# Narrow loads in four marked pieces and stores in halves, in a masked softmax that fills its DMA engines

## The chip, the cores and the metric

The kernel runs on one core of one Trainium2 chip. The metric is the device time of one execution in microseconds; lower is better. Each run has a state: slow, here, when it took over 1.5% longer than the fastest of its kernel, otherwise fast. A "ratio" is the mean time of one kernel's fast runs over the mean of the other's fast runs of the same rounds, so it is not quite the ratio of the medians quoted. The *span* of a profile is some 1.5 to 2.5 us shorter than the time measured for the same execution (154.3 against 155.95 us for the kernel before).

## The reference

```python
batch, heads, seq_q, seq_k = 16, 8, 256, 256       # x: float32; lengths: int, 128 to 255
for b in range(batch):
    length = lengths[b]
    masked = x[b, :, :, :length].copy()
    masked = masked - np.max(masked, axis=-1, keepdims=True)
    exp_masked = np.exp(masked)
    result[b, :, :, :length] = exp_masked / np.sum(exp_masked, axis=-1, keepdims=True)
# the rest of result is zero
```

A batch is 2048 rows of 256 floats: 2.10 MB in and 2.10 MB out. On chip it lies as 128 partitions of 16 rows. Only the first `length` columns of a row have to be read, but all 256 have to be written.

## The kernel before

Eight slots of 16 rows a partition hold the batches. Batches 0 to 3 are loaded whole by SyncE. Batches 4 to 15 are loaded by GpSimd, which reads the length, walks a tree of branches to the smallest width that covers it (160, 168, ... 240 or 256 columns), and issues one DMA of that width.

```python
slots = 8
ahead = 4
widths = list(range(160, 248, 8))
...
def parts(b):                       # how the store of batch b is cut
    if b == 0:
        cuts = [0, nt]              # nt = 16 rows a partition
    elif b < 8:
        cuts = [0, half, half + quarter, nt]
    elif b != batch - 3:
        cuts = [0, half, nt]
    else:
        cuts = [0, nt]
    return [slice(i, j) for i, j in zip(cuts, cuts[1:])]
...
for b in range(batch):              # SyncE: the stores
    s_b = s_st[b % 2]
    for s in parts(b):
        nc.sync.wait_ge(s_out, 2 * b + (s.stop - 1) // half + 1)    # divided
        if b >= 2 and s.start == 0:
            nc.sync.wait_ge(s_b, 64 * (b // 2 + 1))                 # store b-2 done
        nc.sync.dma_start(out=out_f[b, :, s, :], in_=xt[:, b % slots, s, :]
            ).then_inc(s_b, 16 * ((s.stop - s.start) // quarter))
...
with nc.Fori(0, (batch - ahead) // 2, 1, engines=[POOL]) as q:      # GpSimd: the loads
    for par in range(2):
        n = 2 * q + (ahead + par)
        v_len = length(POOL, word[0:1, bass.ds(2 * n, 1)])
        with nc.gpsimd.If(q >= 1):
            nc.gpsimd.wait_ge(s_sw[par], 16 * q)    # load n-2 has landed
            nc.gpsimd.wait_ge(s_st[par], 64 * q)    # store n-8 is done: the slot is free
        pick(v_len, bass.ds(n, 1), bass.ds(n % slots, 1), par, widths + [seq_k])
...
# VectorE: mask(b) waits for the load; ScalarE: exp with row sums, row by row;
# VectorE: divide(b, half) = reciprocal and multiply; a divided half may be stored
```

The softmax here doesn't subtract the row's maximum and nothing guards it: scores larger than these inputs give would overflow.

## Time and profile before

| | kernel before |
|---|---|
| time, median of 3 | 156.11 us (155.78 to 156.81) |
| span of the profiled execution | 154.3 us |
| DMA queues q0 (GpSimd's loads) and q1 (the rest), share of 16 engines' span | 32.2% and 66.0% |
| VectorE, ScalarE busy | 75%, 68% |
| VectorE's wait for loads | 14.0 us in all |
| last load landed (the last completion event of its semaphore) | 132.7 us |

The page's parts for this kernel are shown in the prediction. The list of waits of SyncE's queue, which issues the stores (who waits, on whom; us in total, times, longest):

```profile
SPq L119 <- DMA out_dram<-xt: 91.7, 14, 9.6
SPq L117 <- DVE xt L222: 14.9, 1, 14.9
SPq L120 <- DVE xt L222: 12.6, 9, 3.3
```

SyncE nearly always waits for an earlier store (91.7 us) and rarely for VectorE (12.6 us after the first batch). So there is a stock of finished batches that queue for the DMA engines. The end of the chain of waits (start in us, duration, what):

```profile
115.19 17.53 DMA xt<-in_x_dram
...
132.95 2.35 DVE xt L195
...
142.77 2.29 DVE xt L222
```

The last load, issued at 115.19 us, lands at 132.7; the mask and four multiplications follow, the last ending at 145.1 us. What lies between 145.1 and 154.3 is the rest of that stock being written. When the last load landed, 8.1 MB of the 33.6 MB of output was still to be stored (counted from the packet records).

### The profile page before, as it was taken

What the parts mean: (1) busy time and instruction counts of PE and PEld (TensorE: products, weight loads), DVE (VectorE), ACT (ScalarE), POOL (GpSimd) and SP (SyncE); (2) the same over time, 40 slices, a digit from 0 to 9 for tenths busy, and PEclk for the clock granted to TensorE, in tenths of its full rate; (3) what the DMA queues carried; (4) which work ended last, traced back from release to release, by engine and by line L of the source; (5) the groups of instructions that cost most, each with busy time, mean ns of one, the idle gap of its engine ahead of it and who ended that gap; (6) DMA issues with size and microseconds to landing.
All of it is one profiled execution on the core that took longest, in us unless ns stands there. A gap on an engine that the chain in (4) does not pass through costs nothing.

```text
span 154.3 us, 1325 instructions
## 1 busy us (share of the span) xinstructions
PE 0.2 (0%) x1; PEld 0.1 (0%) x1; DVE 115.4 (75%) x84; ACT 105.2 (68%) x514; POOL 19.0 (12%) x25
## 2 busy tenths in 40 slices
PE   0000000000000000000000000000000000000000
PEld 0000000000000000000000000000000000000000
DVE  1339999952999696988969696969698692599500
ACT  3097799992592969779595959596877907988000
POOL 4910031000320200202011020202010000000000
DMA  4999999999999999999999999999999999999993
GB/s 117 427 450 420 437 365 409 400 408 452 407 406 390 415 404 417 412 413 415 405 419 413 414 412 405 416 416 420 417 416 423 418 431 435 418 444 418 423 431 130
DMA packets 10132, 62.08 MB, mean 402 GB/s; under 512 B 866, under 2 KB 962, under 8 KB 6290
## 3 DMA queue, kind: packets, MB, share of 16 engines
q1 hardware_dynamic: 6048, 41.95, 66.0%
q0 software_dynamic: 4080, 20.12, 32.2%
q14 instruction: 2, 0.02, 0.0%
q10 hardware_dynamic: 2, 0.00, 0.0%
HBM read 28.51 MB, written 33.55 MB: 402 GB/s over the span
## 4 chain that ended last, share of the span: by engine, by line
DMA 54%; DVE 25%; issue 7%; ACT 5%; ACTq 2%; SPq 1%; POOLq 1%; DVEq 0%
DMA xt<-in_x_dram 33%; DMA out_dram<-xt 21%; DVE xt L222 14%; DVE xt L195 9%; ACT xt L251 5%; ACTq L251 1%; DVE inv_sum L219 1%; SPq L109 1%; POOLq L99 0%; SPq L120 0%; SPq L111 0%; DVEq L212 0%; POOLq L130 0%; POOLq L135 0%; ACTq L246 0%
## 5 line engine op out<-in xcount | busy, mean ns | idle before, releaser
L251 ACT ACTIVATE xt<-xt x256 | 102.3, 401 | 35.2 <-DVE xt L195 35.2
L222 DVE TENSOR_TENSOR xt<-xt,inv_sum 128x2048 f32<-128x2048 f32 x32 | 73.4, 2292 | 1.1
L195 DVE SCALAR_TENSOR_TENSOR xt<-down,len_s,xt 128x2048 f32<-128x2048 f32 (+1 forms) x17 | 37.8, 2221 | 14.1 <-DMA xt<-in_x_dram 14.0
L251 ACT ACTIVATION_READ_ACCUMULATOR xt<-xt x256 | 47.9, 187 | 0.0
L130 POOL DMA_DIRECT2D xt<-in_x_dram x12 | 12.8, 1064 | 94.6 <-issue 48.7
L219 DVE RECIPROCAL inv_sum<-row_sum 128x8 f32<-128x8 f32 x32 | 6.3, 198 | 12.1 <-ACT xt L251 12.1
L149 POOL MEMSET xt<- 128x1536 f32 x4 | 5.3, 1386 | 1.1 <-DVE len_s L186 1.1
L243 ACT ACT_TABLE_LOAD x1 | 1.3, 1283 | 1.6 <-SPq L81 1.6
L178 DVE TENSOR_SCALAR down<-iota_i 128x256 f32<-128x256 int32 x1 | 0.3, 297 | 1.6 <-POOL iota_i L141 1.6
L183 DVE CAST len_b<-word 1x16 bf16<-1x16 int32 x1 | 0.2, 164 | 0.4 <-DMA word<-in_lengths_dram 0.4
L186 DVE TENSOR_SCALAR len_s<-len_f 128x16 f32<-128x16 f32 x1 | 0.2, 174 | 0.4 <-PE len_f L165 0.4
L141 POOL IOTA iota_i<- 128x256 int32 x1 | 0.3, 332 | 0.6 <-SPq L81 0.6
L146 POOL MEMSET seed<- 1x1 f32 x2 | 0.3, 162 | 0.0
L243 ACT ACTIVATE warm<-const-float32-0.0 128x1 f32<-128x1 f32 x1 | 0.2, 203 | 0.0
L144 POOL MEMSET ones<- 1x128 bf16 x1 | 0.2, 194 | 0.0
L165 PE MATMUL len_f<-len_b,ones 1*128 1x16 bf16 x1 | 0.2, 168 | 2.6 <-DVE len_b L183 2.6
L274 POOL MEMSET const-float32-0.0<- 128x1 f32 x1 | 0.1, 98 | 0.3 <-issue 0.3
L165 PEld LDWEIGHTS len_f<-len_b,ones 1*128 1x128 bf16 x1 | 0.1, 97 | 2.6 <-POOL ones L144 2.6
L274 POOL MEMSET const-float32-1.0<- 128x1 f32 x1 | 0.1, 98 | 0.0
L274 POOL MEMSET const-bfloat16-1.0<- 128x1 bf16 x1 | 0.1, 98 | 0.0
L274 POOL MEMSET const-uint8-127<- 128x1 uint8 x1 | 0.1, 98 | 0.0
L274 POOL BASE_LOAD x1 | 0.0, 17 | 0.1
## 6 DMA issues: line engine op xcount, KB each, us to landing
out_dram<-xt SPq DMA_DIRECT2D x21, 1024.0 KB
out_dram<-xt SPq DMA_DIRECT2D x14, 512.0 KB
xt<-in_x_dram SPq DMA_DIRECT2D x3, 2048.0 KB, 16.0
xt<-in_x_dram POOLq DMA_DIRECT2D x3, 1728.0 KB, 16.5
out_dram<-xt SPq DMA_DIRECT2D x2, 2048.0 KB
xt<-in_x_dram POOLq DMA_DIRECT2D x2, 2048.0 KB, 18.4
xt<-in_x_dram POOLq DMA_DIRECT2D x2, 1600.0 KB, 16.7
xt<-in_x_dram POOLq DMA_DIRECT2D x2, 1280.0 KB, 14.5
```

Source lines behind the costliest of these rows:

```text
L109: nc.sync.dma_start(out=xt[:, 0, s], in_=x_f[0, :, s]).then_inc(s_ld[h], 16)
L130: nc.gpsimd.dma_start(out=xt[:, slot, :, :w], in_=x_n[:, n, :, :w]).then_inc(s_sw[par], 16)
L141: nc.gpsimd.iota(iota_i, pattern=[[1, seq_k]], base=0, channel_multiplier=0).then_inc(s_iota, 1)
L146: nc.gpsimd.memset(seed[:, par : par + 1], 0.0).then_inc(s_st[par], 64)
L149: nc.gpsimd.memset(xt[:, b, :, low:], 0.0).then_inc(s_fill, 1)
L165: nc.tensor.matmul(len_f, lhsT=ones, rhs=len_b, start=True, stop=True).then_inc(s_lenf, 1)
L195: return nc.vector.scalar_tensor_tensor(out=t, in0=down[:, None, lo:hi].to_broadcast([P, s.stop - s.start, hi - lo]), scalar=len_s[:, b : ...
L219: step(nc.vector.reciprocal(out=inv_sum[:, b, s], in_=row_sum[:, b, s]))
L222: nc.vector.tensor_tensor(out=t, in0=t, in1=inv_sum[:, b, s, None].to_broadcast([P, half, seq_k]), op=ALU.mult,).then_inc(s_out, 1)
L243: nc.scalar.activation(out=warm, in_=nc.const_aps.tensor(0.0, (P, 1), F32), func=EXP)
L251: ins = nc.scalar.activation(out=e, in_=e, func=EXP, accum_out=sum_h[:, bass.ds(i, 1), j])
L274: nc = _bacc.Bacc("TRN2", target_bir_lowering=False, num_devices=1)
```

## The change

The intent: fewer and longer DMA packets. Each narrow load is cut into four pieces of four rows, 32 runs for each of the 16 DMA engines, each piece marked as a single packet, which should also let the loads get a larger turn beside the stores. With that, the stores in quarters, which had been there to give the loads their turn, become halves.

```diff
+    piece = 32 * 16 // P            # 4 rows
+    pieces = nt // piece            # 4
...
-        if b == 0:
-            cuts = [0, nt]
-        elif b < 8:
-            cuts = [0, half, half + quarter, nt]
-        elif b != batch - 3:
-            cuts = [0, half, nt]
-        else:
-            cuts = [0, nt]
+        cuts = [0, nt] if b == 0 else [0, half, nt]
...
-                    out=xt[:, slot, :, :w], in_=x_n[:, n, :, :w]
+                    out=xt_g[:, slot, g, :, :w], in_=x_g[:, n, g, :, :w], single_packet=True
                 ).then_inc(s_sw[par], 16)
...
-                    nc.gpsimd.wait_ge(s_sw[par], 16 * q)
+                    nc.gpsimd.wait_ge(s_sw[par], 16 * pieces * q)
                     nc.gpsimd.wait_ge(s_st[par], 64 * q)
-                pick(v_len, bass.ds(n, 1), bass.ds(n % slots, 1), par, widths + [seq_k])
+                with nc.Fori(0, pieces, 1, engines=[POOL]) as g:
+                    pick(v_len, bass.ds(n, 1), bass.ds(n % slots, 1), bass.ds(g, 1), par, widths + [seq_k])
...
-                nc.vector.wait_ge(s_sw[b % 2], 16 * ((b - ahead) // 2 + 1))
+                nc.vector.wait_ge(s_sw[b % 2], 16 * pieces * ((b - ahead) // 2 + 1))
```

More of the change, by code (lines that the diff above doesn't have):

```diff
@@ L122, with pick @@
                 ).then_inc(s_b, 16 * ((s.stop - s.start) // quarter))
-        def pick(v, n, slot, par, ws):
+        def pick(v, n, slot, g, par, ws):
             if len(ws) == 1:
@@ L135, in pick @@
             with nc.gpsimd.If(v <= ws[m]):
-                pick(v, n, slot, par, ws[: m + 1])
+                pick(v, n, slot, g, par, ws[: m + 1])
             with nc.gpsimd.Else():
-                pick(v, n, slot, par, ws[m + 1 :])
-        x_n = x_f.rearrange("b p t c -> p b t c")
+                pick(v, n, slot, g, par, ws[m + 1 :])
+        x_g = x_f.rearrange("b p (g j) c -> p b g j c", j=piece)
+        xt_g = xt.rearrange("p s (g j) c -> p s g j c", j=piece)
         nc.gpsimd.iota(
@@ L157 @@
                 with nc.gpsimd.If(q >= 1):
-                    nc.gpsimd.wait_ge(s_sw[par], 16 * q)
+                    nc.gpsimd.wait_ge(s_sw[par], 16 * pieces * q)
                     nc.gpsimd.wait_ge(s_st[par], 64 * q)
-                pick(v_len, bass.ds(n, 1), bass.ds(n % slots, 1), par, widths + [seq_k])
+                with nc.Fori(0, pieces, 1, engines=[POOL]) as g:
+                    pick(
+                        v_len,
+                        bass.ds(n, 1),
+                        bass.ds(n % slots, 1),
+                        bass.ds(g, 1),
+                        par,
+                        widths + [seq_k],
+                    )
         nc.tensor.wait_ge(s_ones, 1)
```

## The prediction

> **What bounds the kernel now.** I first read the head of the page and its parts 1 to 3, to see which resource is full.
>
> ```profile
> span 154.3 us, 1325 instructions
> ...
> PE 0.2 (0%) x1; PEld 0.1 (0%) x1; DVE 115.4 (75%) x84; ACT 105.2 (68%) x514; POOL 19.0 (12%) x25
> ...
> DMA  4999999999999999999999999999999999999993
> GB/s 117 427 450 420 437 365 409 400 408 452 407 406 390 415 404 417 412 413 415 405 419 413 414 412 405 416 416 420 417 416 423 418 431 435 418 444 418 423 431 130
> DMA packets 10132, 62.08 MB, mean 402 GB/s; under 512 B 866, under 2 KB 962, under 8 KB 6290
> ...
> q1 hardware_dynamic: 6048, 41.95, 66.0%
> q0 software_dynamic: 4080, 20.12, 32.2%
> ```
>
> The DMA row is 9 or more in every slice between the first and the last. Queue q1 carries the first four loads and all stores, q0 the twelve narrow loads that GpSimd issues; together 98.2% of 16 engines' span, 151.5 us of work. VectorE and ScalarE, 75% and 68% busy, are fed by it and feed it. So the kernel is bound by the throughput of the DMA engines, not by a compute engine.
>
> The chain of waits names the same thing but must be read with care: it goes through a load at 20 to 37 us, through VectorE and ScalarE until 81 us, then through stores and a load until 133 us. That is who released whom; all that time the DMA engines were also busy with something else. I therefore asked for stretches. The columns after the busy times are granted clock, DMA share and GB/s:
>
> ```profile
> 2.50:20.00 17.50, 0.17 (x1) 0.10 (x1) 11.24 (x9) 10.70 (x52) 5.33 (x4) 1.00 1.01 423
> 20.00:30.00 10.00, 0.00 (x0) 0.00 (x0) 9.90 (x8) 10.00 (x52) 1.85 (x2) 1.00 0.98 385
> ...
> 40.00:120.00 80.00, 0.00 (x0) 0.00 (x0) 69.22 (x50) 61.58 (x304) 9.75 (x9) 1.00 1.02 413
> ...
> 132.00:151.00 19.00, 0.00 (x0) 0.00 (x0) 11.97 (x9) 9.41 (x48) 0.00 (x0) 1.00 1.01 429
> ```
>
> The share never falls below 0.98, but the rate differs: 413 GB/s where loads and stores mix, 429 where only stores of 8 KB packets are left. (Shares over 1 mean that neighbouring packets overlap by 1 to 2%.) Full engines moving fewer bytes means a cost per packet. The packet records in the trace give it. A packet of 16384 B takes 611 ns at the median, one of 8192 B 313 ns, one of 4096 B 162 ns. From 8192 to 16384 B that is 298 ns for 8192 B, 27.5 B/ns; the shorter ones sit 9 to 12 ns above a line of 27.2 B/ns through zero (16 engines at that rate are 435 GB/s). The load packets of 4320 to 4800 B take 171 to 191 ns, the same 12 to 14 ns above it, and those of 4704 B 194 ns.
>
> [...] beside 8192 B store packets, load packets of about 4500 B take 0.35 to 0.39 of the busy time (4.5/(4.5+8.2) is 0.35); beside the 4096 B packets of the stores in quarters they take 0.51 to 0.56 at times (0.52 expected); at about 125 us the 16384 B packets of the last, full-width load take 0.67 beside 8192 B stores.
>
> [...]
>
> [...] Here the records show 4320 to 4800 B, the smallest number of whole rows (5 to 7) that reaches 4 KB. [...]
>
> **The change part by part.**
>
> Loads. A piece is 4 rows on 128 partitions, so each of 16 engines gets 8 partitions x 4 rows = 32 descriptors[...]. As a single packet that is 20 to 32 KB. The ten narrow loads had 3472 full packets and 160 remainders; their records sum to 39.7 us of 16 engines. After: 10 x 4 x 16 = 640 packets; their 15.93 MB at 435 GB/s are 36.6 us, plus 640 x 12 ns / 16 = 0.5: 37.1 us. Saved: 2.6 us. The two full-width loads go from 256 packets of 16384 B to 128 of 32768 B: saved 0.1. Completion records (4 B, 9 ns, 16 per DMA) rise from 12 x 16 = 192 to 768: cost 576 x 9 / 16 = 0.3 us.
>
> Stores. Batches 1 to 7 had one half in two quarters: 7 x 2 x 128 = 1792 packets of 4096 B at 162 ns (18.2 us of 16 engines by the records) become 896 of 8192 B at 313 ns, 17.5: saved 0.7. Batch 13 goes from one piece to halves: 128 x 611 ns becomes 256 x 313 ns: cost 0.1. Six fewer stores save 96 completion records, 0.05.
>
> Sum by the records: 2.6 + 0.1 - 0.3 + 0.7 - 0.1 + 0.05 = 3.0 us of DMA work. Because records overlap, I check it with an effective cost: 62.08 MB at 435 GB/s is 142.7 us; the engines work from about 2.7 to 151.6 us, 148.9; the difference of 6.2 us x 16 / 10132 packets is 9.8 ns for a packet of any size. Packets go from 4080 + 6048 = 10128 to 1536 + 5184 = 6720 (q0: 768 data and 768 completions; q1: 512 of 16384 B, 4096 of 8192 B, 576 completions): 3408 x 9.8 / 16 = 2.1 us. So 2.1 to 3.0, and I take 2.5. All of it lies on the path that sets the end, because the engines never idle.
>
> GpSimd. The program's order shows that the tree of branches is now walked four times a load. Before, from the end of the wait to the start of the transfer's descriptor work went 1.3 us (113.86 to 115.19 in the chain). The descriptor work was 1.15 us for 2048 rows and 0.56 us for the 128 long ones, so about 0.7 us for 512 rows. A piece each 1.0 to 1.4 us is a load each 4 to 5.6 us, where one is needed each 9 us (3.7 MB a batch at 415 GB/s). GpSimd is 12% busy. This is beside other work.
>
> Order of service. A 26 KB load packet against an 8 KB store packet gives loads about 26/(26+8.2) = 0.76 of the engines instead of 0.35 to 0.56. A load of 1.6 MB that took 16 us to land should take 5 to 8 us from its first piece. VectorE's wait before the mask goes:
>
> ```profile
> DVE xt L195 <- DMA xt<-in_x_dram: 14.0, 4, 4.8
> ```
>
> These 14 us are in the chain, but they buy little: compute comes earlier, and the stores then queue behind full engines. VectorE without that wait would finish around 131 to 134 us instead of 145 (batch 0 is divided at 18.6 us in the timeline, and 15 more batches take 7.5 us each: 2.35 + 2 x 2.29 + 2 x 0.2 and small gaps), with stores still in the queue.
>
> **The rivals.**
>
> 1. "Removing the load waits shortens the end by up to 14 us." For it: the chain runs through those loads and compute. Against it: bytes are unchanged, and 62.08 MB at 435 GB/s plus 2.7 us of head and 2.7 of end (151.6 to 154.3) is a span of 148.1, a time of about 150 (the profiled run took 155.95 us with a span of 154.3); no order of service goes below that. I give a little to it: the stretch of 20 to 30 us has only 385 GB/s (413 would save 0.7 us), and a better mixture may recover part of it.
>
> 2. "Loads now starve the stores." The stores get 24% while loads run; a load waits for the store eight batches earlier, and the store of a batch for that of two batches before. If loads and stores took turns instead of overlapping, there could be holes when neither is allowed. Against it: two loads of different parity and two batches of stores may be outstanding, and by 60 us VectorE has produced some 11 MB to store (five batches and a half at that pace). I expect turns but no holes; were each batch to lose 0.3 us, the time would be about 157.5.
>
> 3. "The single packet doesn't help or hurts": 32 descriptors of 640 to 1024 B could each cost as much as a packet. Against it: load packets of 5 rows stand as little above the line as a store packet of one run (12 ns each); only those with rows of 672 B are at 21 ns. If the cost is by row, only the 0.7 us of the stores is won, less the 0.3 of completions and 0.1 of batch 13: 155.8. If long read packets hold up the write side, the time could pass 157.
>
> 4. GpSimd's issue becomes the limit of the loads. At 5.6 us a load it is not, and if a piece took 2.3 us it would be; stores would still fill the engines, so about 154 to 155.
>
> **Range and chances.** 156.1 - 2.5 = 153.6 us. The record sum gives 153.1, the effective cost 154.0; with some of rival 1 it is 152.4, with rivals 3 or 2 156 to 157. The range that should hold it 8 times in 10 is 152.0 to 155.8. Faster by over 2% means below 153.0, just past the record sum: 0.32. Within 2%: 0.64. Slower (above 159.2): 0.04.
>
> **What would show it right or wrong.** Right: q0 about 1536 packets and q1 about 5184, with 20.12 and 41.95 MB; the sum of the shares of q0 and q1 about 148.5 us; the mixed stretch of 40 to 120 us above 418 GB/s with the DMA share still near 1; the wait of the mask for loads below 7 us; the final stores still queued when VectorE ends. Rival 2 would show as slices below 9 in the DMA row; rival 3 as packets of 20 to 32 KB that take clearly more than size / 27.2 + 12 ns, or q0 keeping some 4000 packets (the mark has no effect); rival 4 as GpSimd's busy time tripled and loads spaced by issue. My estimate is wrong if packet counts fall as said and the mixed rate stays at 413: then the cost is not one of packets but of mixing reads and writes.

## The result, and the profile after

The changed kernel takes 170.45 us (median of 4, 170.01 to 171.47) against 156.43 us of the kernel before in the same rounds; the ratio is 1.0911, with a 95% interval of 1.0846 to 1.0975. It is slower by 9%, outside the predicted range of 152.0 to 155.8 us. The outputs are correct.

The page of the changed kernel, parts 1 to 3 (busy us and share by engine; tenths in 40 slices; DMA queues with packets, MB, share of 16 engines):

```profile
span 167.7 us, 1790 instructions
...
PE 0.2 (0%) x1; PEld 0.1 (0%) x1; DVE 115.9 (69%) x84; ACT 105.2 (63%) x514; POOL 40.7 (24%) x61
...
DMA  4999999999999999999999999999999999940895
GB/s 135 444 426 434 434 385 409 413 383 421 415 342 374 410 328 420 419 422 372 388 408 417 413 402 411 398 341 330 299 410 414 414 330 428 425 197 0 344 420 237
DMA packets 10884, 62.08 MB, mean 370 GB/s; under 512 B 1346, under 2 KB 1794, under 8 KB 6274
...
q1 hardware_dynamic: 5184, 41.95, 60.9%
q0 software_dynamic: 5696, 20.12, 33.1%
```

Three things differ from what was foreseen. First, q0 has 5696 packets, more than before (4080), not the 1536 of literal single packets. The records have the same full packets as before, 4096 to 4800 B, and each piece adds a remainder: 32 rows of 864 B make six packets of five rows (4320 B) and one of two (1728 B). Second, the DMA row has a hole near the end (4, 0), while VectorE and ScalarE have no more work than before. Third, many slices have full DMA engines and still only 299 to 374 GB/s.

The waits of VectorE, and those of SyncE's queue, for the changed kernel:

```profile
DVE xt L200 <- DMA xt<-in_x_dram: 30.8, 10, 9.7
```

```profile
SPq L116 <- DVE xt L227: 120.3, 30, 12.2
SPq L113 <- DVE xt L227: 14.8, 1, 14.8
SPq L115 <- DMA out_dram<-xt: 10.0, 5, 3.2
```

The roles are exchanged. SyncE now waits for VectorE before nearly every store (120.3 us) and hardly for the DMA (10.0 us); VectorE waits 30.8 us for loads instead of 14.0. There is no stock of finished batches any more. The end of the chain shows what that costs:

```profile
136.88 13.11 DMA xt<-in_x_dram
...
150.23 2.35 DVE xt L200
...
160.04 2.29 DVE xt L227
```

The stretches before and after the last load landed follow, with the columns that the prediction explains (the last three are clock, DMA share and GB/s):

```profile
137.00:150.00 13.00, 0.00 (x0) 0.00 (x0) 5.60 (x4) 7.92 (x40) 0.41 (x1) 1.00 0.90 374
150.00:168.00 18.00, 0.00 (x0) 0.00 (x0) 11.97 (x9) 6.53 (x33) 0.00 (x0) 1.00 0.56 233
```

The last load lands at 150.0 us, 17.3 later than before, and only 4.2 MB are left to store: batches 14 and 15, of which neither is divided yet (the division of batch 14 stands behind the mask of batch 15 in VectorE's order). From then on the DMA engines are 56% busy, because VectorE first has to mask and divide.

The account of the 13.4 us of span: the packets took 94.0% of 16 engines' 167.7 us, 157.6 us, which is 6.1 more than the 151.5 before (98.2% of 154.3); and the engines stood idle for 8.7 us instead of 1.2 between 20 us and the last data packet (added up over 1-us stretches filled to less than 95%). 6.1 + 7.5 = 13.6. Of the signs that the prediction had named for being right, only the 5184 packets of q1, the unchanged bytes and full engines from 40 to 120 us came true: q0 has 5696 packets, the shares of q0 and q1 sum to 157.6 us and not 148.5, and that stretch moves 386 GB/s (at a DMA share of 1.01) and not over 418.

### The profile page after: what moved, and what is told of

It reads as the page before. It is cut to its first block, busy times and chain, and to the rows that moved or that the text cites. A ratio compares the mean times of both kernels' runs of the same rounds, so it can differ in the third digit from the quotient of the medians.

```text
span 167.7 us, 1790 instructions
## 1 busy us (share of the span) xinstructions
PE 0.2 (0%) x1; PEld 0.1 (0%) x1; DVE 115.9 (69%) x84; ACT 105.2 (63%) x514; POOL 40.7 (24%) x61
## 3 DMA queue, kind: packets, MB, share of 16 engines
q1 hardware_dynamic: 5184, 41.95, 60.9%
q0 software_dynamic: 5696, 20.12, 33.1%
## 4 chain that ended last, share of the span: by engine, by line
DMA 49%; issue 21%; DVE 18%; POOLq 7%; POOL 1%; SPq 1%; DVEq 0%
DMA xt<-in_x_dram 43%; DVE xt L227 12%; DMA out_dram<-xt 6%; DVE xt L200 6%; POOLq L126 4%; POOLq L131 2%; POOL xt L126 1%; POOLq L157 1%; DVE inv_sum L224 1%; SPq L105 0%; POOLq L95 0%; SPq L107 0%; POOLq L133 0%; DVEq L217 0%; POOLq L154 0%
## 5 line engine op out<-in xcount | busy, mean ns | idle before, releaser
L200 DVE SCALAR_TENSOR_TENSOR xt<-down,len_s,xt 128x2048 f32<-128x2048 f32 (+1 forms) x17 | 37.8, 2223 | 30.9 <-DMA xt<-in_x_dram 30.8
L126 POOL DMA_DIRECT2D xt<-in_x_dram x48 | 34.5, 718 | 94.6 <-issue 79.8
```

What stands on the lines that cost most here:

```text
L126: nc.gpsimd.dma_start(out=xt_g[:, slot, g, :, :w], in_=x_g[:, n, g, :, :w], single_packet=True).then_inc(s_sw[par], 16)
L200: return nc.vector.scalar_tensor_tensor(out=t, in0=down[:, None, lo:hi].to_broadcast([P, s.stop - s.start, hi - lo]), scalar=len_s[:, b : ...
```

## The experiments

Three theories were set against each other first. A, the loop of loads: a load is issued only after load n-2 has landed, so whatever lengthens a landing delays all later loads. B: the mark does the harm. C: the four pieces do it by themselves. The parts of the change were run apart, on one chip, beside the kernel before (156.09 us there).

### e1_halves: the stores alone

```diff
 kernel before
-        if b == 0: ... (quarters in batches 1 to 7, batch 13 whole)
+        cuts = [0, nt] if b == 0 else [0, half, nt]
```

> The kernel before with the stores of batches 1 to 15 in halves; loads stay whole. Theory A (the loop of loads: load n is issued only after load n-2 has landed, so what lengthens a landing delays every later load; the mark does nothing): store packets of 8192 B instead of 4096 B cut the loads' share of the engines from about 0.52 to 0.35 in the first half, landing times rise, and the time is 158 to 163 us. Theory B (the single-packet mark alone does the harm): 155 to 156, because 0.7 us of packet time is saved. Theory C (the four pieces alone): 155 to 156 too.

Measured: 159.3 us, ratio 1.0199 (1.0179 to 1.0220; unclear by the 2% line, but clear of no change). The part that should have saved 0.7 us costs 3.2. The share that the loads have of the DMA engines falls: over the 1-us stretches from 45 to 115 us in which both queues are active, the median share of q0 is 0.44 in the kernel before and 0.37 here. The last load lands at 139.5 us instead of 132.7, and SyncE's wait for VectorE grows from 12.6 to 95.0 us:

```profile
SPq L113 <- DVE xt L215: 95.0, 27, 7.8
```

B and C fall as sole causes.

### e2_pieces and e3_pieces_marked: the pieces alone, without and with the mark

```diff
 changed kernel
-        cuts = [0, nt] if b == 0 else [0, half, nt]
+        (the cuts of the kernel before)
-    ..., in_=x_g[:, n, g, :, :w], single_packet=True     # e2 only; e3 keeps the mark
+    ..., in_=x_g[:, n, g, :, :w]
```

> The kernel before with the loads in four unmarked pieces; stores as before (quarters in batches 1 to 7). Theory A: the four issues take GpSimd some 5.5 us from first to last, part of it hidden, so 160 to 167 us. Theory B: within 1% of before. Theory C: as the changed kernel, about 170.

> As e2 with each piece marked as a single packet. Theory A: the same as e2 within 1%, and again load packets of 4320 to 4800 B with remainders. Theory B: slower than e2 by 5% or more.

Measured: e2 166.59 us, ratio 1.0643 (1.0576 to 1.0711); e3 165.11 us, ratio 1.0575 (1.0514 to 1.0635). One of e2's four runs, 168.03 us, was slow and is in the median but not in the ratio; by the means of fast runs (166.22 against 156.18 us) the pieces cost 10.0 us. The intervals overlap, and q0 has 5696 packets of the same sizes in both, so the mark did nothing that can be seen.

### e4_pieces_halves: the changed kernel without the mark

```diff
 changed kernel
-    ..., in_=x_g[:, n, g, :, :w], single_packet=True
+    ..., in_=x_g[:, n, g, :, :w]
```

> The changed kernel without the mark. Theory A: the same as the changed kernel within 1%, about 170 us, with the same packets. Theory B: 156 to 160. Theory C: about 170.

Measured: 169.42 us, ratio 1.0848 (1.0822 to 1.0874), with the same packet counts as the changed kernel, whose own interval overlaps. B is dead: the mark is worth under 1% in either direction. The ratios of e1 and e2 multiply to 1.0855, close to e4's 1.0848.

### e5_leaf: the tree of widths walked once a load

```diff
 e2
-        pick(...) inside a loop over the four pieces
+        for h in range(pieces):     # in the leaf of the tree, unrolled
+            r = slice(h * piece, (h + 1) * piece)
+            nc.gpsimd.dma_start(out=xt[:, slot, r, :w], in_=x_n[:, n, r, :w]).then_inc(s_sw[par], 16)
```

> As e2 (four unmarked pieces, quarters kept), but the tree of widths is walked once and its leaf issues the four pieces one after the other. If the time between pieces (1.85 us in e2) is mainly the walk and the loop, it falls to some 0.8 to 1.1 us, the span from first to last issue from 5.4 to about 3 us, loads land 2 to 3 us sooner and the time is 160 to 163 us. If the descriptor work of a piece is what counts (0.75 us), it stays within 1% of e2, 166 us.

Measured: 184.93 us, ratio 1.1836. A miss, and by much. The issues within a load did come closer (2.2 us from first to fourth in most loads, for 5.4), but the lines of the DMA queues of this kernel show why it was no clean test of that:

```profile
q0 software_dynamic: 5696, 20.12, 33.1%
q14 instruction: 29, 0.24, 0.3%
```

There are 29 entries of instruction transfers, against 2 in the kernel before and in the changed kernel. GpSimd's program is 274 instructions long here, 160 in the changed kernel and 132 before (counted in the built programs, without register moves and plain semaphore instructions). That the longer program brings the transfers, and that they are what delays the loads, is the author's inference from these counts and was not shown; e8 below has the same sign (14 transfers).

### e6_two: two pieces of eight rows

```diff
 e2
-    piece = 32 * 16 // P
+    piece = 64 * 16 // P
```

> As e2 with two pieces of eight rows. Loop theory: the span from first to last issue is about 2 us, and the time is 159 to 162 us. If the stall of some 5 us at the 34th issue in e2 to e4 (second piece of load 12) comes from a count of DMAs, it is gone, as there are 24[...].

Measured: 163.9 us, ratio 1.0495 (1.0471 to 1.0520), a little above the expectation (its profiled execution was the fastest of five, 161.9 us). Half the pieces keep most of the loss. The stall in load 12 stayed: 6.1 us before its second piece, which is the 18th issue here and the 34th in e2, so the number of DMAs issued does not decide it.

### e7_gate_before and e8_gate_after: four load semaphores for two

```diff
 kernel before (e7), changed kernel (e8)
-        s_sw = [sem("s_sw0"), sem("s_sw1")]
+        s_sw = [sem(f"s_sw{k}") for k in range(4)]
-        with nc.Fori(0, (batch - ahead) // 2, 1, engines=[POOL]) as q:
-            for par in range(2):
+        with nc.Fori(0, (batch - ahead) // 4, 1, engines=[POOL]) as q:
+            for par in range(4):        # load n waits for load n-4, not n-2
-                    nc.gpsimd.wait_ge(s_st[par], 64 * q)
+                    nc.gpsimd.wait_ge(s_st[par % 2], 128 * q + 64 * (par // 2))
...
```

> The kernel before with four load semaphores in place of two: load n waits for load n-4 and for the store of batch n-8, no longer for load n-2. Loop theory: the kernel before already has full engines, so only the wait for loads in VectorE and the end of the compute move; 152 to 156 us. If the gate on load n-2 set its end, 148 to 151 us.

> The changed kernel with the same four load semaphores, everything else (pieces, mark, halves) as changed. Loop theory: the issue of the pieces is hidden behind earlier loads and the loss is mostly undone: 154 to 160 us. If the loss comes from the transfers themselves (smaller load packets' share, remainders, GpSimd's issue rate), it stays above 165 us.

Measured: e7 156.54 us, ratio 1.0020 (0.9988 to 1.0052). The wait for load n-2 does not bind the kernel before: the last load is issued at 101.9 us instead of 115.2 and still lands only at 131.6. e8: 174.59 us, ratio 1.1150 (1.1068 to 1.1231), slower than without the relaxation. It is confounded like e5: its program on GpSimd is 298 instructions, and 14 instruction transfers are in its profile.

### e9_lean_before, e10_lean_after and e11_lean_gate_after: a shorter tree

The lengths of this draw need only six of the eleven narrow widths. With only these the bytes are the same and GpSimd's program shrinks (92, 110 and 198 instructions), so that the gate can be tested again.

```diff
 kernel before (e9), changed kernel (e10), e8 (e11)
-    widths = list(range(160, 248, 8))
+    widths = [160, 168, 184, 200, 216, 224]
```

> Control: the kernel before with only the six narrow widths that these lengths use in the tree (160, 168, 184, 200, 216, 224), so the bytes loaded are the same and GpSimd's program is shorter. 155 to 156.5 us, as before, on any theory.

> The changed kernel with the same six widths. If the stall of 5 us at GpSimd's first issue (20.8 to 25.7 us) is a fetch of instructions that the longer program brings forward, the first issue comes at about 21 us and the loads land some 4 us sooner; with fewer branches a piece takes perhaps 1.7 us: 162 to 167 us. If the stall has another cause, above 168.

> e10 with four load semaphores (no wait for load n-2). The same gate in e8 came with a program of 298 instructions on GpSimd and repeated instruction fetches; here it has 198. Loop theory: the next load's pieces are issued without waiting and the time falls below e10 by 4 us or more, to 156 to 162 us. If the gate is not what counts, within 1% of e10.

Measured: e9 156.01 us, ratio 0.9977 (0.9958 to 0.9997), so the shorter tree is neutral in the kernel before. e10 167.78 us (one of four runs, 168.72, was slow; the mean of the fast ones is 167.19), ratio 1.0750 (1.0703 to 1.0796), just above the expected range: the first stall is gone, GpSimd's first issue comes at 21.1 us, near the 20.7 of the kernel before, and not at 25.7, but only about 1.6 points of the 9 came back. In the changed kernel an 8192 B instruction transfer ran at 23.9 us, inside the 4.9 us of that stall; that this transfer is its cause is inferred from this and from e10, not shown directly.

e11 166.31 us, ratio 1.0620 (1.0587 to 1.0653). It is 1% faster than e10, not the 4 us that theory A asked for. This decided against A as the main cause, because in e11 all issues are done by 117 us, as its chain of waits shows (start, duration):

```profile
117.20 29.68 DMA xt<-in_x_dram
```

The last piece was in the queue for nearly 30 us. In e11 GpSimd's issue and its waits no longer set the late landing; the loads lay in the queue and got too small a share of the engines.

### e12_shift: where the second stall sits

```diff
 e2
-    widths = list(range(160, 248, 8))
+    widths = list(range(160, 240, 8)) + [252]
```

> As e2 (four unmarked pieces, quarters kept), with a width of 252 in place of 240 in the tree, so that loads 5 and 15 are also 32 short descriptors a piece on each engine (33 with the completion) instead of 8 long ones. [...] If it belongs to load 12 or its branch, it stays at the second piece of load 12. Time within 2% of e2.

Measured: 167.06 us, ratio 1.0644 (1.0576 to 1.0711), as e2. The profiled run of e12, 168.25 us, was slow; its profile is used only for the order of events. GpSimd's issues in e2 (start, duration, engine, idle before):

```profile
99.41 0.75 POOL L133 DMA_DIRECT2D xt<-in_x_dram  x1 [4.58 <-issue]
106.44 0.76 POOL L133 DMA_DIRECT2D xt<-in_x_dram  x1 [6.28 <-issue]
```

and in e12:

```profile
93.98 0.75 POOL L133 DMA_DIRECT2D xt<-in_x_dram  x1 [0.85 <-issue]
99.26 0.76 POOL L133 DMA_DIRECT2D xt<-in_x_dram  x1 [4.52 <-issue]
```

In e2 the second piece of load 12 (the 34th issue) stalls for 6.3 us before it starts, in e12 the fourth piece of load 11 (the 32nd) for 4.5, so the stall belongs neither to load 12 nor to its branch. The stalls end 0.6 to 0.7 us after an earlier load has landed (load 11 at 105.8 us, load 10 at 98.6). Their cause was not shown: in e13 and e16 below, which issue the same pieces, the 34th comes 2.3 us after the one before it, only some 0.6 us late.

### A new theory, and four runs to test it

A table of all profiles up to here gave the key: the span against the landing of the last load.

| run | last load landed, us | span, us | difference |
|---|---|---|---|
| e1 | 139.5 | 157.2 | 17.7 |
| e6 | 142.2 | 159.9 | 17.7 |
| e3 | 144.8 | 162.4 | 17.6 |
| e2 | 145.9 | 163.6 | 17.7 |
| e10 | 146.7 | 164.4 | 17.7 |
| e11 | 146.9 | 164.5 | 17.6 |
| e4 | 149.6 | 167.2 | 17.6 |
| changed kernel | 150.0 | 167.7 | 17.7 |
| e8 | 155.0 | 172.6 | 17.6 |
| e5 | 165.6 | 183.3 | 17.7 |
| kernel before | 132.7 | 154.3 | 21.6 |
| e7 | 131.6 | 154.8 | 23.2 |

From the last landing a fixed chain follows: mask, exp, four divisions and the last store, 17.7 us. If the last load lands early enough (before and e7), the stores still queue when this chain is done and the sum of all packets sets the end; if it lands later than about 154.3 - 17.7 = 136.6 us, each further microsecond is paid in full. So theory S: what counts is how soon the loads get through, which is the share that they have of the engines. The records, in stretches of 0.5 us from the first issue to the last landing (a queue counts as present in a stretch when its packets take more than about a tenth of the engines' time; if any packet counts, the changed kernel has 11.5 us of loads alone and not 19.0):

| | no load in the engines | loads alone | both | load rate while both |
|---|---|---|---|---|
| kernel before | 8.0 us | 0.5 us | 103.5 us | 192 GB/s |
| e1 | 10.5 us | 5.5 us at 368 GB/s | 103.0 us | 175 GB/s |
| e11 | 9.0 us | 17.0 us at 342 GB/s | 100.0 us | 142 GB/s |
| changed kernel | 13.5 us | 19.0 us at 313 GB/s | 92.0 us | 153 GB/s |

The two sides of the share are sizes of packets in turns. In stretches in which both queues are busy throughout, the records of the two kernels show about one packet of q0 for each packet of q1. In the kernel before there are 443 and 444 from 112 to 124 us (load packets mostly of 4320 B, stores of 8192 B), 150 and 145 from 73 to 76 us (4416 B beside mostly 4096 B) and 86 and 91 from 126 to 131 us (16384 B beside 8192 B); in the changed kernel 465 and 466 from 64 to 76 us (mostly 4320 and 4480 B beside 8192 B). Completions are included; without them the first and the last are 426 and 396, and 402 and 418. A load with rows of 864 B gives each engine 128 rows, 110592 B. Whole, they go in 25 packets of five rows, one of three and a completion (a record of 4 B, counted here as a turn): 27 turns of 4096 B on average. In pieces, they go in 4 x (6 + 1 + 1) = 32 turns of 3456 B. From one packet for one, the loads' shares are estimated at 0.33 and 0.30 beside stores of 8192 B (4096/(4096 + 8192) and 3456/(3456 + 8192)), and at 0.50 and 0.46 beside 4096 B.

### e13_gate_pieces: pieces, always queued, with the old store cuts

```diff
 e11
-        cuts = [0, nt] if b == 0 else [0, half, nt]
+        (the cuts of the kernel before: quarters in batches 1 to 7, batch 13 whole)
-    ..., single_packet=True
+    ...
```

> Four unmarked pieces, six widths, four load semaphores, stores as in the kernel before (quarters in batches 1 to 7, batch 13 whole); against e11 only the store cuts (and the mark) differ. Theory S: the share of loads rises in the first half, the last load lands at 136 to 142 us instead of 146.9, the span is that plus 17.7, the time 156 to 161 us. If pieces themselves cost the time, whatever the store packets: 164 to 167.

Measured: 164.12 us, ratio 1.0498 (1.0477 to 1.0519). The direction is right and the size is not: the last load landed at 144.0 us, not at 136 to 142. By number this run lies with the rival ("pieces themselves", 164 to 167). It left the matter to e16.

The record has a closer pair than e11, though. e7 and e13 differ only in the pieces (and in the widths, neutral by e9), and neither waits for load n-2. The pieces move the last landing from 131.6 to 144.0 us and the load rate beside stores from 190 to 166 GB/s, 13% less, where the turns give an estimated 8 to 11%; the packets' own time grows by only 0.8 us. So pieces lose share whatever the stores are, and the expectation had left that out of its range.

### e14_gate_halves: whole loads, always queued, with halves

```diff
 e1
+    (six widths, and the four semaphores of e7)
```

> Whole loads, six widths, four load semaphores, all stores but the first in halves; against e1 the loads are always queued. Theory S: the share stays that of e1, only the time without a load shrinks (10.5 us in e1, 7.0 in e7), the last load lands at 135 to 139 us, time 155 to 159 us. If the wait for load n-2 was what hurt e1: 153 to 155, better than before, as the stores' packets are fewer.

Measured: 159.57 us, ratio 1.0203 (1.0183 to 1.0223), the same as e1 (1.0199), and slightly above the range. Loads that are always queued gain nothing beside stores in halves. The last load landed at 139.7 us. The median share is 0.37 here with whole loads, 0.33 in e11 with pieces: the difference that the turns gave.

### e15_quarters: smaller store packets beside whole loads

```diff
 kernel before, six widths
-        (its cuts)
+        cuts = [0, nt] if b == 0 else [0, quarter, half, half + quarter, nt]
```

> The kernel before with six widths and all stores but the first in quarters (4096 B packets throughout). Theory S: the share of loads is about 0.5 to the end, the last load lands at 124 to 130 us, and the span is no longer tied to it but to the work of the engines, which grows by some 1.5 us of packets: 155.5 to 158 us. If the landing of the last load mattered in the kernel before, it gets faster, 150 to 154.

Measured: 158.3 us, ratio 1.0115 (1.0091 to 1.0140). The last load landed at 119.4 us, earlier still than expected, with a median share of 0.54. The time did not follow; it was 0.3 us over the range. Here the engines' own work sets the end: more packets, and idle only 2.1 us.

### e16_gate_pieces_quarters: smaller store packets beside pieces

```diff
 e13
-        (the cuts of the kernel before)
+        cuts = [0, nt] if b == 0 else [0, quarter, half, half + quarter, nt]
```

> e13 with all stores but the first in quarters. Theory S: with a share near 0.5 to the end the last load lands at 130 to 138 us, so that most of the loss of the pieces is gone: 155 to 158.5 us. If pieces themselves cost the time: within 1% of e13 and above 163.

Measured: 158.49 us, ratio 1.0130 (1.0107 to 1.0154), at the upper end of what S expected and far from e13. The median share is 0.49 (0.54 in e15, again the difference of the turns); the last load landed at 129.0 us. Its page and SyncE's waits show full engines to the end, and a stock of stores:

```profile
DMA  4999999999999999999999999999999999999991
```

```profile
SPq L115 <- DMA out_dram<-xt: 79.2, 14, 8.7
...
SPq L116 <- DVE xt L227: 9.6, 11, 3.4
```

The 48 pieces cost nothing measurable against e15's whole loads (158.3 us on the same chip, there with two semaphores) once the stores' packets are small. They still move the last landing by 9.6 us (119.4 to 129.0), but both landings come before the 136.6 us at which it begins to cost.

### e17_after_quarters: one line of the changed kernel

```diff
 changed kernel
-        cuts = [0, nt] if b == 0 else [0, half, nt]
+        cuts = [0, nt] if b == 0 else [0, quarter, half, half + quarter, nt]
```

> The changed kernel with one line changed: all stores but the first in quarters (4096 B packets). Theory S: beside 4096 B packets the loads keep about half of the engines, the last load lands at 131 to 138 us instead of 150.0, GpSimd's stalls of 5 us stay, and the time is 157.5 to 161 us. If the wait for load n-2, the mark or the longer program carry a large part of the loss by themselves: 163 to 168.

Measured: 159.75 us, ratio 1.0225 (1.0191 to 1.0258; the verdict by the 2% line is unclear). With its mark, twelve leaves, stalls and wait for load n-2 in place, the changed kernel loses 2.3% instead of 9.1% when its stores are cut in quarters. The last load lands at 139.1 us, a little outside the expected 131 to 138, and loads alone fall from 19.0 us to 2.5. SyncE's waits show part of the stock of stores again (120.3 and 10.0 us in the changed kernel):

```profile
SPq L116 <- DVE xt L227: 50.1, 22, 6.3
SPq L115 <- DMA out_dram<-xt: 48.1, 12, 6.5
```

(The rule of the last landing holds on: e13 144.0 + 17.7, e14 139.7 + 18.2, e17 139.1 + 18.5 us; the two that land near the limit have some stock of stores left.)

No version beat the kernel before. Its last load lands some 4 us earlier than needed and its engines idle for 1.2 us, so better balance has nothing left to give there, and none of these edits reduced the work of the engines below its own.

## Why the prediction was wrong

In short: the step that failed is the overlap, "the engines never idle", and behind it the share of the loads. The prediction expected the loads to take about 0.76 of the engines beside the stores; they took 0.33 to 0.37, where they had 0.44 before, and came too late to keep a stock of stores. The last load landed 17.3 us later; 3.9 us of that were room, and the other 13.4 are the added span.

**What bounds the kernel.** Right for the kernel before, and confirmed by e7: an earlier issue of loads moved nothing. Wrong was the step from there, "All of it lies on the path that sets the end, because the engines never idle." That they never idle is no property of the kernel but of a balance: loads early enough that a stock of stores remains. The change broke the balance and the engines idled for 8.7 us.

**Loads, "As a single packet that is 20 to 32 KB".** This step failed first. The mark was taken literally, a piece as one packet, before any run had shown it. The records show packets of 4096 to 4800 B as before and remainders, 4928 data packets and not 768. The 2.6 us saved did not exist. The prediction named this sign ("q0 keeping some 4000 packets (the mark has no effect)") in rival 3, but priced it at 155.8 us. What was missing there is the next point.

**Order of service, "loads about 0.76 of the engines".** The share was 0.33 to 0.37 at the median. The prediction had measured the shares itself: 0.35 to 0.39 beside 8192 B packets, 0.51 to 0.56 beside 4096 B. With a mark of no effect, the store halves alone move batches 1 to 7 from the second figure to the first, and the pieces with their remainders take another 0.04 to 0.05 (e14 and e11, e15 and e16). It priced the store cuts as packets saved ("saved 0.7") and never as share lost. e1 measured that: +3.2 us.

**"These 14 us are in the chain, but they buy little."** True only towards earlier. e15 showed it: 13 us earlier landing, no gain. Towards later the price is full once the last landing passes some 136.6 us, and the changed kernel's lies at 150.0. Nothing in the prediction looked at how much room was left (132.7 against 136.6: 4 us). This was the step that would have turned the sign.

**GpSimd, "a piece each 1.0 to 1.4 us".** The prediction's own two figures, 1.3 us of walk and 0.7 of descriptor work (the DMA instruction on GpSimd, 0.75 us for most pieces in the changed kernel), add up to 2.0. Together it was 1.6 to 2.0 us in the timeline, about 5 to 6 us from first to last issue in most loads, and two stalls of about 5 us were not foreseen. They were not the main cause: without the first stall the ratio went from 1.0911 to 1.0750 (e10), and without the wait for load n-2 to 1.0620 (e11). The completions grew to 768 as said; their cost in time is small, but by the estimate of the turns each is a turn.

**Rival 2, "Loads now starve the stores".** Its sign came, slices below 9 in the DMA row, but from the opposite cause: stores overtook the loads, ran out of finished batches, and left the loads alone in the engines for some 19 us at about 315 GB/s. Rival 1's floor was never tested, and rival 4 (issue as limit of the loads, stores filling the engines) does not hold either: with issue done by 117 us the last load of e11 still landed at 146.9.

**What the sum became.** By the means of fast runs, stores in halves cost 3.1 us (e1) and pieces 10.0 us (e2); with the mark within noise they make 13.1 of the changed kernel's 14.2. Neither is a fixed cost. Pieces moved the last landing by 7 to 13 us in each of five pairs (before and e2, e1 and e4, e7 and e13, e14 and e11, e15 and e16), and this cost time only where it passed the limit. Still open is why loads alone run so slowly. In the changed kernel two stretches stand side by side (clock, DMA share and GB/s last):

```profile
43.60:46.60 3.00, 0.00 (x0) 0.00 (x0) 2.96 (x3) 1.19 (x6) 1.33 (x2) 1.00 1.03 419
46.60:49.60 3.00, 0.00 (x0) 0.00 (x0) 2.97 (x3) 3.00 (x17) 0.94 (x2) 1.00 1.02 317
```

In the first, load 5 runs alone with packets of 4096 B in whole 4 KB runs; in the second, load 6 joins with rows of 672 B, whose packets of 4704 B took 234 ns at the median there, against 194 in the kernel before. It is not these rows alone: with loads alone, packets of 4320 B took 192 ns at the median in e1 (171 beside stores) and those of 4416 B 215 ns in e11 (174), with the engines full. The longer packets are part of the 6.1 us of added work. No run separated row length from address pattern.

## What to carry to other kernels

Where DMA queues share full engines, as here, look at the size of the packets in each: going from quarters to halves in seven batches took the loads' median share from 0.44 to 0.37 (e1), so a change that makes store packets longer must be priced as a loss of share for the loads too. Find out how far the last load is from setting the end (its landing plus the fixed chain behind it, against the span): inside that room (4 us here) delays were free, beyond it they cost one for one. Check a request such as a packet mark in the packet records before building on it (q0 had 5696 packets with the mark and without), and look at the number of instruction transfers after each change that lengthens a program on GpSimd (2 in the changed kernel, 29 in e5 and 14 in e8).
